# Four gate tiles of a two-group encoder step as two pairs by seven products, with two edits in its attention

## The chip, the cores and the metric

The kernel runs on one core of one Trainium2 chip. The metric is the device time of one execution in microseconds (us). A core has five engines with a queue of instructions each: TensorE (PE, matrix products; its weight loads are shown as PEld), VectorE (DVE), ScalarE (ACT), GpSimd (POOL) and SyncE (SP), which issues the DMAs here. An engine takes its instructions in the order of the program and waits for another through semaphores. PE writes its results to PSUM, which has eight banks; DVE and ACT read them there.

## The reference

Two layers of a streaming encoder work on 1152 tokens: 1024 of a prompt and 8 x 16 of running streams, which also have 256 cached keys and values each. The parts that matter here, for one layer:

```python
h = jnp.einsum('btd,de->bte', x, w_in)
px, pg, q, k, v, ag, ga, gb = jnp.split(h, IN_SPLITS, axis=-1)
...
o = prompt_diff_attention(q, k, v, lam)      # per head: (softmax(q1 k1) - lam * softmax(q2 k2)) v
of = o.astype(jnp.float32)
of = of * lax.rsqrt(jnp.mean(jnp.square(of), -1, keepdims=True) + RMS_EPS)
of = of * subln_w.astype(jnp.float32) * (1.0 - lam_init)
yb = of.astype(x.dtype).reshape(B, T, D_ATT) * jax.nn.silu(ag)
merged = (jax.nn.sigmoid(ga) * jnp.einsum('btc,cd->btd', ya, w_a)
          + jax.nn.sigmoid(gb) * jnp.einsum('btc,cd->btd', yb, w_b))
```

`ag` is the output gate of the attention: 1024 columns, one tile of 128 for each of 8 heads. `ga` and `gb` gate the merge of the two branches, `pg` gates the pooling branch.

## The kernel before

All matrix products of the projections are made in three matmuls on values split into a high and a low part (high x high, high x low, low x high), each over 128 rows of the contraction. A layer has these stages, in this order.

**The V stage** (and, in layer 0, the entry normalisation). It also prepares sums of blocks of x, `t1` to `t4`.

**The pair stage.** `pairs` lists 14 pairs of weight tiles. Two tiles and the two halves of the contraction form a block matrix of 2 x 2; so do the two halves of the contraction and of the tokens. `unit` multiplies them in seven block products in place of eight, for one of two column groups `c` of 288 tokens at a time (`CW`). A block product (`prod`, L595 to L602) is 4 x 3 matmuls of 288 columns, so a pair is 2 x 7 x 12 = 168 matmuls. `keep` and `join` form the sums, and `emit` (L605) finishes a quarter of the result: for a pool gate (`"pg"`) a tanh on ACT, one product on DVE, and a store to DRAM two ticks later. The weights of a pair are added and split in `Weights`, in the order of `plan`.

**The pool stage**: four merge gates (`gates_p2`), the pooling branch, and the product with `w_a`.

**The attention stage.** `attention()` is a generator that goes over `flow`: 8 heads with 9 query tiles each (eight of the prompt, in the order 7, 3, 6, 2, 5, 1, 4, 0, and the decode tile "d"; a tile i has (i+1) x 128 keys). In round j it emits, in this order: the scores of tile j (`s1_tile`, PE into `ps_two`, two buffers; tiles 4 to 7 take one for each map); the transposes of tile j-2 (`s2a_tile`, PE into `bank("tr")`, two buffers, copied to `at` by ACT at L1120); the softmax of tile j (`soft`: DVE's maximum, ACT's exponential); the mix of tile j-1 on DVE (`mix_tile`); the pending squares on ACT; a first `yield f1`; the products of tile j-2 with V (`s2b_tile`) and the copy of its output out of PSUM (`finish`, L1125); a second `yield f2`. For the decode tile `s1_dec`, `mix_dec`, `s2a_dec` and `s2b_dec` take these places.

At each yield the caller emits steps of `filler()`: single steps (three matmuls of 384 columns, L321 to L323, into `bank("lin")`) of the gate tiles in `gate_order`. A tile takes 3 token groups x 8 steps = 24 steps; the last step of a group is followed by ACT's tanh (L975), for the attention's gate by a DVE product (L978), and by a store. How many steps a yield gets is set by

```python
share = (len(gate_order) * NG * KD - REST) / (H * sum(map(sum, STEPS)) + HEAD0)
```

with `NG` 3, `KD` 8, `REST` 28, `H` 8, `HEAD0` 8 and `STEPS` the nine (f1, f2) of a head, 52 in sum. A running sum `due` turns share x f into whole steps. `gate_order` has 16 tiles: the eight of the attention's gate, then eight of `gb`. `g_load` reads a head's gate back from DRAM one head later, for `post_b`.

**The merge stages**: the product with `w_b`, the gating, the product with `w_o` and the normalisation.

Of the kernel before, what the change touches and what calls it, by code (L numbers as in the profile page):

```python
# [11 lines left out]
F32 = mybir.dt.float32  # L12
F32R = mybir.dt.float32r
AF = mybir.ActivationFunctionType
ALU = mybir.AluOpType
AX = mybir.AxisListType

P = 128
# [10 lines left out]
H = 8  # L29
# [3 lines left out]
KD = D // P  # L33
# [7 lines left out]
U_PX, U_PG, U_Q, U_K, U_GA, U_GB, U_AG = 0, 4, 8, 16, 24, 32, 40  # L41
# [23 lines left out]
def trunk(ctx, tc, a):  # L65
    nc = tc.nc
    V, S, G, PE = nc.vector, nc.scalar, nc.gpsimd, nc.tensor
# [3 lines left out]
    small = ctx.enter_context(tc.tile_pool(name="small", bufs=3))  # L71
# [5 lines left out]
    def dr(name, shape):  # L77
        return dram.tile(shape, F32, tag=name, name=name)
# [15 lines left out]
    def later(n, fn):  # L94
        pending.append([n, fn])
# [29 lines left out]
        return t[:, :, g * GW:(g + 1) * GW]  # L125

    gates_p2 = [(2, d) for d in range(KD - MG, KD)]
    gate_order = [(0, d) for d in range(H)] + [(1, d) for d in range(KD)]

    GATE_U = (U_AG, U_GB, U_GA)  # L130
    pairs = []
# [6 lines left out]
        pairs.append(("pg", g, U_PG + g))  # L138
    for d in range(0, KD - MG, 2):
        pairs.append(("ga", d, U_GA + d))  # L140

    plan = []
    for l in range(DEPTH):
# [315 lines left out]
    for l in range(DEPTH):  # L459
# [3 lines left out]
        g_d = dr(f"g_d{l}", [H, P, T])  # L463
# [4 lines left out]
        sg_d = dr(f"sg_d{l}", [4, P, T])  # L468
# [22 lines left out]
        def cols(c, half):  # L491
            o = half * HT + c * CW
            return slice(o, o + CW)
# [35 lines left out]
        for n in range(2 * NT):  # L529
            u, t = n // NT, (TO, TO1)[n // NT][n % NT]  # L530
# [62 lines left out]
        def tt():  # L593
            return p1.tile([P, CW], F32, tag="tt", name="tt", bufs=11)
# [9 lines left out]
        def emit(kind, idx, e, c, half, src, psum):  # L604

            o = cols(c, half)
            if kind == "px":
                if psum:
                    t = tt()
                    S.copy(t, src)  # L610
                    src = t
                g = idx + e
                if half == 1 and c == 1:
                    n = SEQ - o.start
                    later(2, lambda: (dma(u_d[g, :, o.start:SEQ], src[:, :n]),
                                      dma(us_d[g, :, :, HIST:], src[:, n:].rearrange("p (b s) -> p b s", b=DB))))
                    return
                dst = u_d[g, :, o]
            elif kind == "pg":
                t = tt()  # L620
                S.activation(out=t, in_=src, func=AF.Tanh, scale=0.5)
                V.scalar_tensor_tensor(out=t, in0=t, scalar=1.0, in1=src, op0=ALU.add, op1=ALU.mult)
                src, dst = t, sg_d[idx + e, :, o]
            else:
                t = tt() if psum else src
                S.activation(out=t, in_=src, func=AF.Tanh, scale=0.5)
                src, dst = t, ga_d[idx + e, :, o]
            later(2, lambda: dma(dst, src))
# [24 lines left out]
        def unit(kind, idx, c, w, end):  # L653
# [20 lines left out]
            def e2():  # L674
                prod(y_, w["a12"], operand("b21", c), True)
                st[11] = join(y_, s1)
                if kind != "rope":
                    emit(kind, idx, 0, c, 0, st[11], False)
# [9 lines left out]
            def e5():  # L688
                prod(z_, w["s4"], operand("b22", c), False)
                st[12] = join(z_, s2)  # L690
                if kind != "rope":
                    emit(kind, idx, 0, c, 1, st[12], False)
                else:
                    rope(*idx, c, 1, st[12], st[22], False)

            def e6():
                prod(x_, w["s3"], operand("t3", c), False)
                st[22] = join(x_, s5)
                if kind != "rope":
                    emit(kind, idx, 1, c, 1, st[22], False)  # L700
# [20 lines left out]
        for kind, idx, _ in pairs:  # L721
            w = {}
            for c in range(2):
                e = unit(kind, idx, c, w, c == 1)
# [39 lines left out]
        nlam = small.tile([P, 1], F32, tag="nlam", name="nlam", bufs=2)  # L764
# [281 lines left out]
        def start_head(h):  # L1046
            hd = heads[h]
            hd["osb"] = ap.tile([P, 9, P], F32, tag="osb", name="osb", bufs=2)
            hd["ss"] = small.tile([P, 9], F32, tag="ss", name="ss", bufs=2)
            hd["r1"] = small.tile([P, 9], F32, tag="r1", name="r1", bufs=2)  # L1050
            G.memset(hd["r1"][:, 8:9], 1.0)

        def s1_tile(h, i):

# [45 lines left out]
        def mix_tile(h, i):  # L1100
            hd = heads[h]
            pt, ls_ = hd["P", i]
            r2 = small.tile([P, 1], F32, tag="ar2", name="ar2")
            V.reciprocal(out=r2, in_=ls_[:, 1:2])  # L1104
            cc = small.tile([P, 1], F32, tag="acc", name="acc")
            V.scalar_tensor_tensor(out=cc, in0=ls_[:, 0:1], scalar=nlam, in1=r2, op0=ALU.mult, op1=ALU.mult)
            V.scalar_tensor_tensor(out=pt[0], in0=pt[1], scalar=cc, in1=pt[0], op0=ALU.mult, op1=ALU.add)  # L1107
            V.reciprocal(out=hd["r1"][:, i:i + 1], in_=ls_[:, 0:1])

        def s2a_tile(h, i):  # L1110
            hd = heads[h]
# [10 lines left out]
            hd["at", i] = ats  # L1122

        def finish(hd, o_ps, i):
            V.tensor_copy(hd["osb"][:, i, :], o_ps)  # L1125

            def square():
                jk = ap.tile([P, P], mybir.dt.bfloat16, tag="jk", name="jk")
                S.activation(out=jk, in_=hd["osb"][:, i, :], func=AF.Square, accum_out=hd["ss"][:, i:i + 1])

            squares.append(square)
# [3 lines left out]
        def do_squares():  # L1135
            while squares:
                squares.pop(0)()

        def s2b_tile(h, i):
            hd = heads[h]  # L1140
            o_ps = bank("tr")[:, :P]
            for b in range(i + 1):
                PE.matmul(o_ps, hd["at", i][b // 4][:, (b % 4) * P:(b % 4 + 1) * P], hd["vt", b // 4][:, b % 4, :],  # L1143
                          start=(b == 0), stop=(b == i))
            finish(hd, o_ps, i)
            del hd["P", i]
# [54 lines left out]
        def s2b_dec(h):  # L1201
            hd = heads[h]
            atl, vn = hd["atl"], hd["qkv"][2]
            o_ps = bank("tr")[:, :P]
            for uu in range(4):
                PE.matmul(o_ps[32 * uu:32 * uu + 32, :], atl[:, 32 * uu:32 * uu + 32], vn, start=True, stop=False,
                          tile_position=(0, 32 * uu))
            for k in range(2):
                for e in range(2):
                    for uu in range(4):  # L1210
                        g, u = divmod(uu, 2)
                        vcv = hd["vc"][g].rearrange("p (j k v) -> p j k v", j=4, k=2)
                        PE.matmul(o_ps[32 * uu:32 * uu + 32, :],
                                  azt[:, k, uu, e * 32:e * 32 + 32], vcv[:, 2 * u + e, k, :],
                                  start=False, stop=(k == 1 and e == 1), tile_position=(0, 32 * uu))
            finish(hd, o_ps, 8)

        def post_a(h):
            do_squares()
            hd = heads[h]  # L1220
            r1, ss, osb = hd["r1"], hd["ss"], hd["osb"]
            f = small.tile([P, 9], F32, tag="wv_", name="wv_", bufs=2)
            V.tensor_tensor(out=f, in0=r1, in1=r1, op=ALU.mult)
            V.tensor_tensor(out=f, in0=f, in1=ss, op=ALU.mult)
            V.tensor_scalar(out=f, in0=f, scalar1=1.0 / P, scalar2=RMS_EPS, op0=ALU.mult, op1=ALU.add)
            G.tensor_tensor(out=f, in0=f, in1=mhalf[:, :9], op=ALU.pow)
            G.tensor_tensor(out=f, in0=f, in1=r1, op=ALU.mult)
            heads[h]["f"] = f
# [50 lines left out]
        def attention():  # L1279
# [6 lines left out]
            def mix(h, i):  # L1286
                mix_dec(h) if i == "d" else mix_tile(h, i)
# [6 lines left out]
            for j in range(len(flow) + 2):  # L1294
# [4 lines left out]
                if n == 0 and h < H:  # L1299
                    start_head(h)  # L1300
# [18 lines left out]
                if 0 < h < H:  # L1319
                    if n == 2:  # L1320
                        post_a(h - 1)
                        g_load(h - 1, 0)
                        g_load(h - 1, 1)
                    if n == 3:
                        post_f(h - 1)
                    if 5 <= n <= 7:
                        post_b(h - 1, n - 5)
                    if n == 5:
                        g_load(h - 1, 2)
                    if n == 7:  # L1330
                        posted.append(h - 1)
# [9 lines left out]
                if h + 1 < H:  # L1341
# [4 lines left out]
                    if n == 8:  # L1346
                        load_vc(h)
                yield f2
            post_a(H - 1)
            post_f(H - 1)  # L1350
            g_load(H - 1, 0)
# [140 lines left out]
        for n, (d, g) in enumerate(chunks):  # L1492
# [14 lines left out]
            t, u = gates.pop(n)  # L1507
# [25 lines left out]
        dst = a["o_y"] if last else x_d[1]  # L1533
# [46 lines left out]
        if last:  # L1580
            t = TO[-1]
# [133 lines left out]
```

## Time and profile before

| | |
|---|---|
| median of 3 runs | 2343.69 us (2340.68 to 2344.43) |
| the profiled execution, its own time | 2339.09 us |
| its span in the trace | 2336.9 us |
| granted TensorE clock, mean | 0.997 |
| pair stage, layer 0 | 125.5 to 439.7 us of the span |
| pool stage, layer 0 | 439.7 to 553.9 |
| attention stage, layer 0 | 553.9 to 956.1 |
| pair, pool and attention stage, layer 1 | 1282.5 to 1596.5, to 1708.6, to 2111.5 |

The profile is of one execution. Durations in its rows are in us where a row begins with a start time (start, duration, engine, line, operation, output<-inputs, shapes, count), and in groups of instructions "busy us, mean ns | idle us before them, and what ended most of it". A matmul's duration overlaps that of the next one, so for PE the distance between starts is what a matmul costs. A row of waits gives the waiting engine and line, what it waited for, the total, the times and the longest.

### The profile page before, as it was taken

Reading aid. Unit: us, or ns where it says so; the run is one execution under the profiler, and the core shown is the slowest. Engines: PE = TensorE matmul, PEld = TensorE weight load, DVE = VectorE, ACT = ScalarE, POOL = GpSimd, SP = SyncE. Lnnn points to the kernel's source line nnn. Section 1 sums busy time; section 2 is a strip of 40 time slices with the busy share of each in tenths; the row PEclk is TensorE's granted clock in tenths of the full one; section 3 lists DMA queues with packets and bytes.
Section 4 is the critical chain, followed back from the end, with each engine's and each line's share of the span. In section 5 each row is a group of like instructions: output and inputs, shape, how many; then the busy total and the mean of one; then the engine's idle time right before and its main releaser. Section 6 shows DMA issues by size and latency. Waiting matters only on the chain.

```text
span 2336.9 us, 39893 instructions
## 1 busy us (share of the span) xinstructions
PE 2284.7 (98%) x14928; PEld 2148.0 (92%) x14928; DVE 1539.3 (66%) x2980; ACT 982.2 (42%) x2177; POOL 302.0 (13%) x312
## 2 busy tenths in 40 slices
PE   7999999999999999999999999999999999999998
PEld 6899999999989998998878999999999899989986
DVE  4478855446888887566424887556378887874755
ACT  8432234323665665433543332342155565653121
POOL 1023310000000000132100333000000010001333
PEclk9999999999999999999999999999999999999999
DMA  6653334656555554586335432455665464536941
GB/s 216 222 126 103 101 102 115 196 151 197 154 172 156 162 170 146 195 290 230 126 122 198 132 101 100 110 123 181 182 180 157 144 201 149 172 124 220 336 155 73
DMA packets 247714, 379.11 MB, mean 162 GB/s; under 512 B 49888, under 2 KB 190176, under 8 KB 247520
## 3 DMA queue, kind: packets, MB, share of 16 engines
q1 hardware_dynamic: 247520, 376.55, 52.3%
q8 instruction: 118, 1.93, 0.4%
q14 instruction: 76, 0.62, 0.1%
HBM read 259.67 MB, written 117.83 MB: 162 GB/s over the span
## 4 chain that ended last, share of the span: by engine, by line
PE 80%; DMA 7%; DVE 6%; ACT 3%; issue 3%; SPq 1%; POOL 1%; DVEq 0%; ACTq 0%; POOLq 0%
PE ps_lin L321 6%; PE ps_lin L323 6%; PE ps_lin L322 6%; PE ps_tr L1143 5%; PE ps_lin L600 5%; PE ps_lin L602 5%; PE ps_lin L601 5%; PE ps_tr L1118 3%; PE ps_tr L601 2%; PE ps_tr L602 2%; PE ps_tr L600 2%; PE ps_lin L336 2%; PE ps_lin L337 2%; PE ps_lin L335 2%; PE ps_two L1085 2%
## 5 line engine op out<-in xcount | busy, mean ns | idle before, releaser
L321 PE MATMUL ps_lin<-xh,wh 128*128 128x384 f32 x952 | 346.4, 364 | 1.5 <-ACT xh L1266 0.9
L322 PE MATMUL ps_lin<-xl,wh 128*128 128x384 f32 x952 | 321.4, 338 | 1.0 <-DVE xl L1269 1.0
L323 PE MATMUL ps_lin<-xh,wl 128*128 128x384 f32 x952 | 321.3, 338 | 0.0
L321 PEld LDWEIGHTS ps_lin<-xh,wh 128*128 128x128 f32 x952 | 180.5, 190 | 6.7 <-issue 2.2
L322 PEld LDWEIGHTS ps_lin<-xl,wh 128*128 128x128 f32 x952 | 180.7, 190 | 2.9 <-DVE xl L1269 2.4
L323 PEld LDWEIGHTS ps_lin<-xh,wl 128*128 128x128 f32 x952 | 179.6, 189 | 0.0
L1120 ACT COPY at<-ps_tr 128x512 f32<-128x512 f32 (+2 forms) x192 | 86.6, 481 | 191.5 <-PE ps_tr L1118 191.3
L1143 PE MATMUL ps_tr<-vt,at 128*128 128x128 f32 x1152 | 150.0, 276 | 0.0
L1143 PEld LDWEIGHTS ps_tr<-vt,at 128*128 128x128 f32 x1152 | 145.8, 191 | 2.0 <-ACT at L1120 2.0
L271 DVE TENSOR_TENSOR wl<-ws,wh 128x1024 fp32r<-128x1024 f32 (+1 forms) x74 | 86.2, 1164 | 75.0 <-ACT wh L266 74.5
L1093 DVE TENSOR_REDUCE anm<-ps_two 128x1 f32<-128x1024 f32 (+3 forms) x128 | 131.2, 1025 | 4.4
L1095 ACT ACTIVATE p<-ps_two,anm 128x1024 f32<-128x1024 f32 (+3 forms) x128 | 122.2, 961 | 25.4 <-DVE anm L1093 22.2
L266 ACT CAST wh<-ws 128x1024 fp32r<-128x1024 f32 (+1 forms) x74 | 74.1, 1002 | 118.5 <-PE ps_lin L322 50.0
L644 POOL TENSOR_TENSOR tt<-tt 128x288 f32<-128x288 f32 x64 | 63.7, 995 | 408.7 <-DVE tt L643 251.0
L1107 DVE SCALAR_TENSOR_TENSOR p<-p,acc 128x1024 f32<-128x1024 f32 (+7 forms) x128 | 104.9, 819 | 4.5
L1075 ACT ACTIVATE p<-ps_two,anm 128x512 f32<-128x512 f32 (+3 forms) x128 | 66.4, 524 | 79.6 <-DVE ar L1104 59.9
L1118 PE MATMUL ps_tr<-ident,p 128*128 128x128 f32 x576 | 85.6, 274 | 6.3 <-ACT at L1120 4.0
L1085 PE MATMUL ps_two<-kh,qs 128*128 128x512 f32 (+3 forms) x256 | 90.1, 355 | 1.4 <-ACT p L1075 1.2
L1086 PE MATMUL ps_two<-kl,qs 128*128 128x512 f32 (+3 forms) x256 | 89.2, 352 | 1.4 <-DVE kl L909 1.4
L663 ACT COPY sb<-ps_lin 128x288 f32<-128x288 f32 x80 | 31.9, 399 | 123.0 <-PE ps_lin L602 117.5
L1118 PEld LDWEIGHTS ps_tr<-ident,p 128*128 128x128 f32 x576 | 68.7, 141 | 12.1 <-ACT at L1120 5.5
L1511 POOL TENSOR_TENSOR mg<-mt 128x384 f32<-128x384 f32 x42 | 60.1, 1436 | 113.3 <-DVE mt L1510 111.7
(522 smaller groups left out, 6855.9 us busy)
## 6 DMA issues: line engine op xcount, KB each, us to landing
ws<-wt SPq DMA_DIRECT2D x96, 512.0 KB, 3.8
mt_d<-th SPq DMA_DIRECT2D x96, 192.0 KB, 2.9
fx<-q_d SPq DMA_DIRECT2D x128, 128.0 KB, 3.3
fx<-o_k SPq DMA_DIRECT2D x128, 128.0 KB, 3.3
st<-ck SPq DMA_DIRECT2D x32, 512.0 KB, 6.6
fx<-cv SPq DMA_DIRECT2D x32, 512.0 KB, 4.8
mt<-mt_d SPq DMA_DIRECT2D x42, 384.0 KB, 5.9
xT_d<-xs SPq DMA_DIRECT2D x36, 256.0 KB, 2.6
```

The source lines that it names most:

```text
L321: PE.matmul(ps, wh[:, k, :], xh[:, k, :], start=(k == 0), stop=False),
L322: PE.matmul(ps, wh[:, k, :], xl[:, k, :], start=False, stop=False),
L323: PE.matmul(ps, wl[:, k, :], xh[:, k, :], start=False, stop=(k == nk - 1)))
L600: PE.matmul(ps, wh[:, k, :], oh[:, k, :], start=first and k == 0, stop=False, **more)
L601: PE.matmul(ps, wh[:, k, :], ol[:, k, :], start=False, stop=False, **more)
L602: PE.matmul(ps, wl[:, k, :], oh[:, k, :], start=False, stop=k == 3, **more)
L1085: PE.matmul(s[:, b, :c], qs[:, ql], kh[:, kc], start=True, stop=False)
L1093: V.tensor_reduce(out=nm[:, m:m + 1], in_=s[:, :, :c], axis=AX.XY, op=ALU.max, negate=True)
L1095: S.activation(out=p[:, :n].rearrange("p (b c) -> p b c", b=2), in_=s[:, :, :c], func=AF.Exp, bias=nm[:, m:m + 1], accum_out=ls_[:, m:m + 1])
L1107: V.scalar_tensor_tensor(out=pt[0], in0=pt[1], scalar=cc, in1=pt[0], op0=ALU.mult, op1=ALU.add)
L1118: PE.transpose(tr[:, j * P:(j + 1) * P], p[:, (b0 + j) * P:(b0 + j + 1) * P], ident)
L1143: PE.matmul(o_ps, hd["at", i][b // 4][:, (b % 4) * P:(b % 4 + 1) * P], hd["vt", b // 4][:, b % 4, :], start=(b == 0), stop=(b == i))
```

## The change

Four of the eight tiles of the attention's output gate, those of heads 0 to 3, leave `gate_order` and become two more pairs at the end of `pairs`, of the new kind "ag". `emit` treats "ag" like "pg", with `g_d` as the destination. `plan` follows both lists, so the eight weight tiles of both layers are loaded, added and split in the pair stage. `share` gets smaller with the length of `gate_order`; `STEPS`, `REST` and `HEAD0` stay. Beside it `finish` copies the attention's output out of PSUM with ACT in place of DVE, and `mix_tile` takes the reciprocals of both row sums in one instruction of two columns, into a tile `r1` that holds both for every query tile, where there were two instructions, one of them behind the mix.

```diff
-    gate_order = [(0, d) for d in range(H)] + [(1, d) for d in range(KD)]
+    gate_order = [(0, d) for d in range(H // 2, H)] + [(1, d) for d in range(KD)]
...
+    for d in range(0, H // 2, 2):
+        pairs.append(("ag", d, U_AG + d))
...
-            elif kind == "pg":
+            elif kind in ("pg", "ag"):
                 t = tt()
                 S.activation(out=t, in_=src, func=AF.Tanh, scale=0.5)
                 V.scalar_tensor_tensor(out=t, in0=t, scalar=1.0, in1=src, op0=ALU.add, op1=ALU.mult)
-                src, dst = t, sg_d[idx + e, :, o]
+                src, dst = t, (sg_d if kind == "pg" else g_d)[idx + e, :, o]
...
-            hd["r1"] = small.tile([P, 9], F32, tag="r1", name="r1", bufs=2)
-            G.memset(hd["r1"][:, 8:9], 1.0)
+            hd["r1"] = small.tile([P, 9, 2], F32, tag="r1", name="r1", bufs=2)
+            G.memset(hd["r1"][:, 8, 0:1], 1.0)
...
-            r2 = small.tile([P, 1], F32, tag="ar2", name="ar2")
-            V.reciprocal(out=r2, in_=ls_[:, 1:2])
+            rr = hd["r1"][:, i, :]
+            V.reciprocal(out=rr, in_=ls_)
             cc = small.tile([P, 1], F32, tag="acc", name="acc")
-            V.scalar_tensor_tensor(out=cc, in0=ls_[:, 0:1], scalar=nlam, in1=r2, op0=ALU.mult, op1=ALU.mult)
+            V.scalar_tensor_tensor(out=cc, in0=ls_[:, 0:1], scalar=nlam, in1=rr[:, 1:2], op0=ALU.mult, op1=ALU.mult)
             V.scalar_tensor_tensor(out=pt[0], in0=pt[1], scalar=cc, in1=pt[0], op0=ALU.mult, op1=ALU.add)
-            V.reciprocal(out=hd["r1"][:, i:i + 1], in_=ls_[:, 0:1])
...
         def finish(hd, o_ps, i):
-            V.tensor_copy(hd["osb"][:, i, :], o_ps)
+            S.copy(hd["osb"][:, i, :], o_ps)
...
-            r1, ss, osb = hd["r1"], hd["ss"], hd["osb"]
+            r1, ss, osb = hd["r1"][:, :, 0], hd["ss"], hd["osb"]
```

## The prediction

> **What bounds the kernel now.** I read the page of the profile first: its list of engines, then the chain that ended last.
>
> ```profile
> PE 2284.7 (98%) x14928; PEld 2148.0 (92%) x14928; DVE 1539.3 (66%) x2980; ACT 982.2 (42%) x2177; POOL 302.0 (13%) x312
> ...
> PE 80%; DMA 7%; DVE 6%; ACT 3%; issue 3%; SPq 1%; POOL 1%; DVEq 0%; ACTq 0%; POOLq 0%
> ```
>
> TensorE (PE) is busy for 98% of the span and makes 80% of the chain. So the time is the sum of the matmul spacings plus what PE stands still. Next I read the busy time by stretches: the last four pairs of the pair stage of layer 0, two at a time, and the attention stage of layer 0 (layer 1 repeats it).
>
> ```profile
> core 0: us, PE busy (x) PEld busy (x) DVE busy (x) ACT busy (x) POOL busy (x), PEclk, DMA share, GB/s
> 350.37:394.89 44.52, 44.52 (x338) 44.52 (x337) 25.41 (x47) 18.38 (x42) 0.00 (x0) 1.00 0.48 130
> 394.89:439.41 44.52, 44.52 (x337) 44.36 (x336) 14.64 (x26) 16.27 (x37) 0.00 (x0) 1.00 0.48 95
> 553.90:956.10 402.20, 395.82 (x2914) 371.19 (x2913) 319.50 (x781) 232.30 (x615) 18.29 (x23) 1.00 0.53 158
> ```
>
> In the pair stage PE never stands and VectorE (DVE) is busy for 25.41 of 44.52 us at most. In the attention PE stands only 6 us of 402, but DVE is busy for 79% of it, and the gate steps in between are what covers DVE's and ScalarE's (ACT's) answers.
>
> **The change part by part: the gate tiles.** Each moved tile leaves 24 steps of three 384-column matmuls out of the attention. The first matmuls of a step and of the third step after it:
>
> ```profile
> 708.74 0.34 PE L321 MATMUL ps_lin<-xh,wh 128*128 128x384 f32 x1
> ...
> 710.30 0.34 PE L321 MATMUL ps_lin<-xh,wh 128*128 128x384 f32 x1
> ```
>
> A step is (710.30 - 708.74) / 3 = 0.52 us. Eight tiles over two layers are 192 steps: 99.8 us off PE. Added are two pairs a layer. Two pairs took 44.52 us, so four take 89.0 us. The product count alone saves 10.8 us. The added pairs' ACT and DVE work is that of the pool gate pairs, the first of the two pair rows, where both fit under PE; if they didn't fit, the excess over 44.52 us would show, and 19 us are spare. The four weight loads and the stores to `g_d` of a layer go through SP's queue in the pair stage instead:
>
> ```profile
> ws<-wt SPq DMA_DIRECT2D x96, 512.0 KB, 3.8
> ```
>
> One tile's load lands in 3.8 us and a pair needs two in 22 us, at a DMA share of 0.48; I cost them at nothing, hidden by the same 44.52 us. Uncovered, each would cost up to its 3.8 us.
>
> A rule of the Trainium skill speaks against this saving. "TensorE: Matmul & The Clock Gate", Back-to-back issue gap, gives a sustained 81 ns a matmul at 128 columns and 131 ns at 512. An estimate on the line between them is 102 ns at 288 columns and 114 ns at 384; then 672 matmuls for 576 would cost 3 us more. The trace disagrees: 44.52 us over 336 is 132 ns and 0.52 us over three is 173 ns, and I go by these.
>
> **What covers less.** The attention issues its gate steps in shares: before, (16 x 24 - 28) / (8 x 52 + 8) = 0.840 of a unit in STEPS, after, (12 x 24 - 28) / 424 = 0.613. A round of one query tile has 3 to 7 units and loses one step of 0.52 us, sometimes two. The load of the engines follows from these rows of the first attention stage (DVE, then ACT):
>
> ```profile
> L1125 DVE COPY osb<-ps_tr 128x128 f32<-128x128 f32 x71 | 20.1, 283 | 20.0 <-PE ps_tr L1143 19.7
> ...
> L978 DVE SCALAR_TENSOR_TENSOR th<-th,ps_lin 128x384 f32<-128x384 f32 x24 | 13.3, 554 | 15.4 <-ACT th L975 15.3
> ...
> L1108 DVE RECIPROCAL r<-als 128x1 f32<-128x1 f32 x64 | 10.0, 156 | 0.0
> ```
>
> ```profile
> L975 ACT ACTIVATE th<-ps_lin 128x384 f32<-128x384 f32 x45 | 22.0, 489 | 11.6 <-PE ps_lin L323 11.6
> ...
> L1120 ACT COPY at<-ps_tr 128x128 f32<-128x128 f32 x16 | 4.3, 268 | 12.9 <-PE ps_tr L1118 12.9
> ```
>
> DVE loses 72 output copies (20.4 us), 64 reciprocals (10.0) and 12 gate products of 0.554 (6.6): 319.5 - 37.0 = 282.5 us. ACT gains 72 copies; the nearest row is its own copy of that shape, 0.268 us, so 19.3, and loses 12 tanh (5.9): 245.7 us. The splitting of four weight tiles, which both lose too, comes on top. PE's stage becomes 402.2 - 49.9 = 352.3 us. At 80% and 70% neither engine is a bound by its sum. The two-wide reciprocal costs what one costs (a width of one more element; bounds 0.156 and twice that), so the chain to the mix keeps its length. What counts is where PE waits for a single answer.
>
> The tightest place comes once a head: query tile 7, then 3, then the decode tile's second half.
>
> ```profile
> 704.92 1.11 ACT L1095 ACTIVATE p<-ps_two,anm 128x1024 f32<-128x1024 f32 x1
> ...
> 706.63 0.40 PE L1066 MATMUL ps_two<-kh,qs 128*128 128x512 f32 x1
> ...
> 707.29 0.28 DVE L1125 COPY osb<-ps_tr 128x128 f32<-128x128 f32 x1
> ...
> 707.56 0.82 PE L1191 MATMUL ps_tr<-ident,p 128*128 128x128 f32 x6
> ...
> 707.60 0.19 ACT L1129 ACTIVATION_READ_ACCUMULATOR jk<-osb 128x1 f32 x1
> ...
> 711.83 0.68 ACT L1075 ACTIVATE p<-ps_two,anm 128x512 f32<-128x512 f32 x1
> ...
> 713.06 0.37 PE L1085 MATMUL ps_two<-kh,qs 128*128 128x448 f32 x1
> ```
>
> Tile 3's scores start at 706.63, in the PSUM that tile 7's first exponential left at 706.03: 0.60 us to spare, of which one step takes 0.52. The second half of the decode transposes (about 707.89, the fourth of six that start from 707.56 at spacings of some 0.11) needs the bank that the output copy frees at 707.57. On ACT that copy stands in its queue behind both exponentials and the square, which end at 707.79, so it ends at 708.06: 0.17 us too late as things stand, and 0.69 with a step gone. Tile 6's second map at 713.06 needs tile 3's second exponential, done at 712.51: 0.55 to spare, again a step. Behind these waits stands all of PE's queue, the gate steps too, since they come later in program order. I see 0 to 1.3 us a head (nothing, or all of the 11 units x 0.227 = 2.5 steps removed there) and take 0.45, as the waits follow each other and the later ones start from a delayed PE: 16 x 0.45 = 7.2 us.
>
> The second place comes every round, between the transposes and the products with V:
>
> ```profile
> 719.83 0.60 PE L1118 MATMUL ps_tr<-ident,p 128*128 128x128 f32 x4
> ...
> 720.46 0.59 ACT L1120 COPY at<-ps_tr 128x512 f32<-128x512 f32 x1 [0.64 <-PE ps_tr L1118]
> ...
> 721.31 0.94 PE L1143 MATMUL ps_tr<-vt,at 128*128 128x128 f32 x7
> ```
>
> Two steps lie between; the copy ends at 721.05, 0.26 us before its use. One step less leaves PE short by 0.26 us. Counting the shares out over the rounds gives 13 a layer that fall from two steps to one (30 go from three to two, which is enough). That is at most 2 x 13 x 0.31 = 8 us, at least 0; long tiles need only their first copy at once, so I take 5.5. For mixes and smaller waits (0 to 4 us) I take 2.
>
> **What is given back.** DVE's output copy makes PE wait today:
>
> ```profile
> PE ps_tr L1191 <- DVE osb L1125: 2.9, 4, 0.7
> PE ps_tr L1118 <- DVE osb L1125: 2.3, 4, 0.7
> ```
>
> These 5.2 us come where DVE is late with the copy. Where ACT is free by then they go, where its exponentials come first they stay. Between 0 and 5.2 I take 3.5. Fewer DVE instructions ahead of a mix help only where DVE is behind; I add nothing.
>
> **Sum.** -10.8 + 7.2 + 5.5 + 2 - 3.5 = +0.4 us. The profiled execution took 2339.09 us (span 2336.9 and 2.2 around it), below the median 2343.69 and the lowest run, 2340.68; applied to the median this is 2344.1, rounded 2344.
>
> **The rivals.** Case A, the forecast: the saved products are spent in new waits of the attention; -4 to +5 us, 2339 to 2349. For it speak the spare times of 0.26 to 0.60 us against a step of 0.52.
>
> Case B, faster: the waits don't add up, because a PE that waited at one place finds the next answer ready, and because DVE, 37 us a layer lighter, answers sooner. Then half of A's waits remain (7 of 14.7) and the relief is 4.4, nearer its upper bound: -10.8 - 4.4 + 7 = -8, 2336. For it: DVE's copies also hold up DVE itself (20 us idle before them). Against: in the rows above DVE had nothing queued ahead of tile 7's reduction.
>
> Case C, slower: the output copy on ACT decides. It waits in ACT's queue behind the exponentials of the round, so the bank pair of the transposes comes free late in each round of tile 7, and weight casts of 1.05 us get ahead of it in others. It decides wherever the exponentials end later than PE's product with V. Price: 0.7 us a head at the decode transposes in place of the part of it in A, 11 us, with 7 for the V products and the rest, and 3 for tile 6, less 10.8: +10, 2354.
> Case D: the change doesn't save what it says. A 288-column matmul at 149 ns (99.8 us / 672) or more would leave nothing of the saving. The pair rows have 132, in every pair, so only the added pairs themselves could be slower. Without the 10.8 the sum is +11, 2355. The Trainium skill's sustained figures, named above, would have it so, at +14; the rows leave it 0.01.
>
> **How the numbers follow.** Chances: A 0.41, B 0.30, C 0.28, D 0.01. About 0.2%, 4.7 us, is what a measurement of this kernel tells from no change: faster 0.30 from B, same 0.41 from A, slower 0.29 from C and D. With no waits and the full relief the bound is -16, with all the steps of the tight place lost and the upper bounds elsewhere it is 20.8 + 8 + 4 - 10.8 = +22; neither end is likely. For 8 in 10 I reach from 2333 (B and 3 more) to 2356 (C and 2 more).
>
> **What would show it.** The pair stage must be 44.5 us a layer longer, and the attention 40 to 45 us shorter; 50 or more would be B, under 37 C. In the waits of PE, the rows that name DVE's `osb` must be gone, with new ones for ACT's `osb` before the decode transposes, for ACT's `at` before V, and for ACT's `p` before the scores. DVE in the attention should fall to about 280 us and ACT rise to about 243. A pair costing more than 22.3 us, or PE waiting for DVE's mix in most rounds, would make the prediction wrong.

## The result, and the profile after

The changed kernel takes 2366.53 us (median of 4 runs, 2365.35 to 2371.44) against 2342.18 for the kernel before on the same chip: a ratio of 1.0106, with a 95% interval of 1.0091 to 1.0121. It is slower by 1.1%, 24.4 us, and outside the range I gave. The profiled execution took 2367.01 us with a span of 2365.2, which is 28.3 more than the 2336.9 of before. The profiled execution of before was a quick one (2339.09 against the median of 2342.18), so some 4 us of these 28.3 are not part of the difference of the medians. The page of the kernel after, its engines and its chain:

```profile
PE 2296.4 (97%) x15024; PEld 2137.1 (90%) x15024; DVE 1532.4 (65%) x2776; ACT 1024.9 (43%) x2373; POOL 299.0 (13%) x312
...
PE 71%; DVE 9%; DMA 8%; ACT 6%; issue 4%; SPq 1%; POOL 1%; DVEq 0%; ACTq 0%; POOLq 0%
```

PE made up 80% of the chain before and makes up 71% now; DVE went from 6% to 9% and ACT from 3% to 6%. More of the end is set by answers that PE waits for. The busy time by stretches shows where. First the kernel before, layer 0: pair stage, pool stage, then (behind the attention, whose row stands in the prediction) merge stage and product with `w_o`.

```profile
125.50:439.60 314.10, 312.09 (x2353) 311.67 (x2352) 208.91 (x380) 104.02 (x217) 67.32 (x66) 1.00 0.41 110
439.60:553.90 114.30, 112.15 (x620) 107.20 (x619) 62.38 (x94) 26.86 (x44) 0.22 (x2) 1.00 0.66 205
...
956.10:1072.50 116.40, 114.88 (x647) 112.59 (x648) 73.28 (x88) 37.23 (x51) 32.78 (x25) 0.99 0.83 280
1072.50:1282.40 209.90, 205.55 (x938) 169.70 (x937) 89.66 (x123) 90.24 (x163) 14.37 (x20) 1.00 0.47 155
```

The same view of the kernel after: the same five stages of layer 0, the attention among them.

```profile
126.20:486.30 360.10, 356.61 (x2689) 356.11 (x2687) 234.80 (x430) 123.20 (x261) 67.31 (x66) 1.00 0.40 109
486.30:603.70 117.40, 112.84 (x612) 107.91 (x613) 63.11 (x95) 26.40 (x43) 0.22 (x2) 0.99 0.64 198
603.70:966.00 362.30, 354.39 (x2628) 319.32 (x2626) 287.21 (x628) 233.70 (x668) 16.43 (x23) 1.00 0.55 163
966.00:1085.60 119.60, 116.72 (x654) 113.74 (x654) 73.44 (x87) 38.28 (x53) 31.32 (x24) 0.99 0.79 269
1085.60:1297.80 212.20, 206.14 (x937) 169.40 (x937) 91.03 (x124) 90.19 (x163) 15.68 (x21) 1.00 0.47 155
```

The first figure behind the stretch is its length. Both layers together, against the forecast:

| stage (us, both layers) | before | after | difference | forecast |
|---|---|---|---|---|
| pair | 628.2 | 721.7 | +93.5 | +89.0 |
| pool | 226.3 | 232.1 | +5.8 | 0 |
| attention | 805.1 | 726.0 | -79.1 | -99.8 + 11.2 = -88.6 |
| merge | 234.0 | 239.1 | +5.1 | 0 |
| product with `w_o`, layer 0 | 209.9 | 212.2 | +2.3 | 0 |
| entry | 125.5 | 126.2 | +0.7 | 0 |
| sum | | | +28.3 | +0.4 |

By the counts of matmuls in the rows, 286 of the layer's 288 left the attention stage as it is cut here, 8 left the pool stage (the few steps ahead of the first scores) and 7 more are in the merge stage, where the rest of the steps runs. At 0.173 us a matmul the attention's waits are 2 x 286 x 0.173 - 79.1 = 19.9 us net, in place of 11.2 (1.7 of them are a stretch at half clock, shown below); the pool stages lost 5.8 + 2.8 = 8.6 and the merge stages 5.1 - 2.4 = 2.7. So of the miss of 27.9 us about 9 lie in the attention's waits and 19 outside it, where I had put nothing.

**The pairs themselves.** The last full four pairs of the kernel after, two at a time:

```profile
352.73:397.25 44.52, 44.52 (x338) 44.52 (x338) 26.56 (x49) 18.84 (x42) 0.00 (x0) 1.00 0.46 134
397.25:441.77 44.52, 44.52 (x338) 44.52 (x338) 20.21 (x35) 18.77 (x42) 0.00 (x0) 1.00 0.52 107
```

A pair takes 22.26 us, as before, with PE busy throughout. What the pair stage has beyond 89.0 stands at its end. There the first weight tile of the pool stage is rounded by ACT (the cast to `wh`) before PE can use it. Before:

```profile
435.19 1.05 ACT L266 CAST wh<-ws 128x1024 fp32r<-128x1024 f32 x1
...
439.63 0.34 PE L321 MATMUL ps_tr<-xh,wh 128*128 128x384 f32 x1
```

After, in the same place:

```profile
485.22 1.98 ACT L268 CAST wh<-ws 128x1024 fp32r<-128x1024 f32 x2
...
486.31 0.44 PE L323 MATMUL ps_tr<-xh,wh 128*128 128x384 f32 x1 [1.48 <-ACT wh L268]
...
487.57 0.44 PE L325 MATMUL ps_tr<-xh,wl 128*128 128x384 f32 x1 [0.64 <-DVE wl L273]
```

The cast began 4.4 us ahead of its use; now PE waits 1.48 us for it, and 0.64 us for `wl` behind it. The block products read their weights from three buffers each of `wh`, `wl` and `fb`, in turn. Before, the stage's last product reads `fb`, and the last one to read `wh` began at 431.44. After, with 16 x 7 = 112 operands in the turn in place of 98, the last three products (from 479.87 on) hold all three `wh`. The code issues no cast for the next stage in the last three products (the `- 3` of experiment 4), so the cast comes only behind them. PE stands 2.1 us per layer. Then the clock drops: of this stretch of the kernel after, the granted clock is the column of 0.50 behind POOL's.

```profile
488.40:491.80 3.40, 3.40 (x12) 3.40 (x11) 0.25 (x1) 0.53 (x1) 0.00 (x0) 0.50 0.89 270
```

Twelve matmuls in 3.40 us are 0.28 us each where 0.17 is the rule. I call this a half-clock stretch; it loses 1.7 us. Apart from the start and end of the program, the kernel before has two such stretches of 3.4 us (at 983 and 2140) and the kernel after five (488, 997, 1304, 1779, 2168). Three more at half speed are 5.1 us, which lie inside the stage differences of the table: one in a pool (488), one in a pair (1304) and one in an attention stage (1779).

**The attention.** PE's weight loads (PEld) run ahead of its matmuls and meet a wait first. Their waits in the first attention stage, before (waiting engine and line, what it waited for: total us, times, longest):

```profile
PEld ps_tr L1191 <- DVE osb L1125: 2.1, 3, 1.0
...
PEld ps_tr L1118 <- DVE osb L1125: 1.8, 3, 0.9
...
PEld ps_tr L1143 <- ACT at L1120: 1.0, 4, 0.3
```

And after, where the line numbers are one or two higher:

```profile
PEld ps_tr L1144 <- ACT at L1121: 7.1, 19, 0.6
...
PEld ps_two L1087 <- ACT p L1171: 4.5, 7, 0.8
PEld ps_tr L1119 <- ACT osb L1126: 3.3, 7, 0.6
PEld ps_tr L1192 <- ACT osb L1126: 2.4, 7, 0.5
```

The rows that name DVE's `osb` are gone; ACT's `osb`, its `at` before V and its `p` before the scores are there, as the prediction wanted them. The second row was not foreseen: the scores of query tile 7 (L1087) wait for the decode tile's exponentials (L1171) of the head before. This is the place in the kernel before, at the start of the third head:

```profile
646.45 1.05 ACT L907 CAST kh<-fx 128x1024 fp32r<-128x1024 f32 x1
...
651.00 0.57 ACT L1170 ACTIVATE p<-ps_two,dnm 128x384 f32<-128x384 f32 x1
...
651.73 0.39 PE L1085 MATMUL ps_two<-kh,qs 128*128 128x512 f32 x1
...
652.65 0.39 PE L1085 MATMUL ps_two<-kh,qs 128*128 128x512 f32 x1
```

And in the kernel after:

```profile
687.39 1.05 ACT L909 CAST kh<-fx 128x1024 fp32r<-128x1024 f32 x1
...
691.25 0.39 PE L1087 MATMUL ps_two<-kh,qs 128*128 128x512 f32 x1
...
691.94 0.57 ACT L1171 ACTIVATE p<-ps_two,dnm 128x384 f32<-128x384 f32 x1
...
692.66 0.50 PE L1087 MATMUL ps_two<-kh,qs 128*128 128x512 f32 x1 [0.32 <-ACT p L1171]
```

The second map's scores take the PSUM buffer that the decode's exponentials leave. Before, the second exponential ended at 651.57 and PE came for the buffer at 652.65, 1.08 us later. After, PE comes for tile 7 only 2.81 us after the cast of `kh` (from its end at 688.44 to 691.25) in place of 4.23 (647.50 to 651.73), and the exponential ends at 692.51, where PE, with 0.23 us from one of these matmuls to the next, would have come at 692.17. The exponential itself is no later: in both kernels it ends 4.07 us after that cast. What changed is that PE, with fewer steps in its queue, comes earlier.

**Where in a round.** From the starts of the matmuls I worked out, for every round of the attention, the distance from its first scores to the next round's, less 0.5195 us for each gate step in it. What is left is the round's own products plus PE's waits. Means over heads 1 to 6 of both layers, as "steps / us left"; the last three columns are kernels of the experiments below.

| round, its scores | before | after | one pair | other STEPS | placed by round |
|---|---|---|---|---|---|
| tile 7 | 4.0 / 2.26 | 3.0 / 2.84 | 3.7 / 2.44 | 4.0 / 2.90 | 4.0 / 2.54 |
| tile 3 | 5.0 / 3.19 | 3.8 / 3.41 | 4.3 / 3.64 | 5.0 / 3.37 | 5.0 / 3.23 |
| tile 6 | 4.3 / 4.44 | 3.2 / 4.54 | 3.7 / 4.52 | 4.0 / 4.32 | 3.0 / 4.37 |
| tile 2 | 5.8 / 2.04 | 4.0 / 2.27 | 5.2 / 2.07 | 4.0 / 2.05 | 4.0 / 2.08 |
| tile 5 | 4.2 / 3.74 | 3.0 / 3.74 | 3.5 / 3.75 | 3.0 / 3.74 | 2.0 / 3.66 |
| tile 1 | 6.0 / 1.85 | 4.5 / 1.86 | 5.2 / 1.82 | 4.0 / 1.82 | 3.0 / 2.00 |
| tile 4 | 4.0 / 3.59 | 3.0 / 3.65 | 3.5 / 3.79 | 3.0 / 4.08 | 3.0 / 4.65 |
| tile 0 | 5.2 / 1.87 | 3.5 / 2.04 | 4.3 / 2.05 | 3.0 / 2.52 | 3.0 / 2.58 |
| decode | 5.2 / 4.03 | 4.0 / 3.92 | 4.5 / 4.04 | 3.0 / 3.73 | 5.0 / 3.79 |
| a head | 43.7 / 27.01 | 32.0 / 28.27 | 37.9 / 28.12 | 33.0 / 28.53 | 32.0 / 28.90 |

After less before is 1.26 us a head, 20 us if taken for all 16 heads: near the net of the attention above. 0.80 of it is in the rounds of tiles 7 and 3, the tightest place of the prediction.

### The profile page after: what moved, and what is told of

Read it like the earlier page. It is cut to its first block, busy times and chain, and to the rows that moved or that the text cites. A ratio compares the mean times of both kernels' runs of the same rounds, so it can differ in the third digit from the quotient of the medians.

```text
span 2365.2 us, 40170 instructions
## 1 busy us (share of the span) xinstructions
PE 2296.4 (97%) x15024; PEld 2137.1 (90%) x15024; DVE 1532.4 (65%) x2776; ACT 1024.9 (43%) x2373; POOL 299.0 (13%) x312
## 4 chain that ended last, share of the span: by engine, by line
PE 71%; DVE 9%; DMA 8%; ACT 6%; issue 4%; SPq 1%; POOL 1%; DVEq 0%; ACTq 0%; POOLq 0%
PE ps_lin L604 6%; PE ps_lin L602 6%; PE ps_lin L603 6%; PE ps_lin L323 4%; PE ps_lin L324 4%; PE ps_lin L325 4%; PE ps_tr L1144 4%; PE ps_tr L603 3%; PE ps_tr L602 3%; PE ps_tr L604 3%; PE ps_lin L338 2%; PE ps_lin L339 2%; PE ps_lin L337 2%; PE ps_tr L1119 2%; DMA mt_d<-th 1%
## 5 line engine op out<-in xcount | busy, mean ns | idle before, releaser
L323 PE MATMUL ps_lin<-xh,wh 128*128 128x384 f32 x760 | 282.0, 371 | 4.5 <-ACT wh L268 1.5
L324 PE MATMUL ps_lin<-xl,wh 128*128 128x384 f32 x760 | 257.4, 339 | 2.7 <-DVE xl L1270 2.7
L325 PE MATMUL ps_lin<-xh,wl 128*128 128x384 f32 x760 | 257.1, 338 | 0.6 <-DVE wl L273 0.6
L323 PEld LDWEIGHTS ps_lin<-xh,wh 128*128 128x128 f32 x760 | 144.2, 190 | 10.6 <-ACT wh L268 3.5
L324 PEld LDWEIGHTS ps_lin<-xl,wh 128*128 128x128 f32 x760 | 144.8, 191 | 5.2 <-DVE xl L1270 4.7
L325 PEld LDWEIGHTS ps_lin<-xh,wl 128*128 128x128 f32 x760 | 143.6, 189 | 1.0 <-DVE wl L273 1.0
L273 DVE TENSOR_TENSOR wl<-ws,wh 128x1024 fp32r<-128x1024 f32 (+1 forms) x66 | 77.6, 1179 | 68.6 <-ACT wh L268 68.2
L268 ACT CAST wh<-ws 128x1024 fp32r<-128x1024 f32 (+1 forms) x66 | 65.4, 996 | 130.1 <-PE ps_lin L324 53.6
L1087 PE MATMUL ps_two<-kh,qs 128*128 128x512 f32 (+3 forms) x256 | 91.7, 361 | 5.2 <-ACT p L1171 2.5
L665 ACT COPY sb<-ps_lin 128x288 f32<-128x288 f32 x96 | 38.3, 399 | 129.4 <-PE ps_lin L604 125.2
```

The lines of the kernel that those rows point to most:

```text
L323: PE.matmul(ps, wh[:, k, :], xh[:, k, :], start=(k == 0), stop=False),
L324: PE.matmul(ps, wh[:, k, :], xl[:, k, :], start=False, stop=False),
L325: PE.matmul(ps, wl[:, k, :], xh[:, k, :], start=False, stop=(k == nk - 1)))
L1087: PE.matmul(s[:, b, :c], qs[:, ql], kh[:, kc], start=True, stop=False)
```

## The experiments

All ratios are against the kernel before, run on the same chip.

**1. The parts alone.** Three kernels, each with one part of the change on the kernel before. The gate tiles alone (`gate_order`, `pairs`, `emit`):

> Only the four gate tiles are moved to the pair stage; the copy of the attention's output stays on VectorE and both reciprocals stay apart. Theory cover (the steps missing in the attention uncover waits that were hidden, and the pair stage ends with the wrong weight buffers free): nearly all of the 24 us of the whole change stays, 2360 to 2368 us, and the attention stage of layer 0 is 360 to 364 us long, as in the changed kernel (362.3). Theory copy (ScalarE's copy, queued behind exponentials and ahead of casts, is what uncovers the waits): the attention falls to 352 to 356 us and the time to 2340 to 2352 us.

2372.56 us, ratio 1.0134 (1.0115 to 1.0152), above both expectations. Its profiled attention stages, 363.4 and 365.7 us, are 1 to 2 us longer than the changed kernel's: the cover theory's sign. The output copy alone:

```diff
-            V.tensor_copy(hd["osb"][:, i, :], o_ps)
+            S.copy(hd["osb"][:, i, :], o_ps)
```

> Only the copy of the attention's output moves from VectorE to ScalarE; the gate tiles stay in the attention. Theory cover: the 5.2 us that TensorE waits for VectorE's copy go and little comes in their place, 2337 to 2343 us. Theory copy: 5 us or more of new waits a layer, 2350 to 2357 us, with ScalarE's output copy named among the waits of TensorE.

2338.03 us, ratio 0.9984 (0.9974 to 0.9993). Its waits in the first attention stage:

```profile
PEld ps_tr L1118 <- ACT osb L1125: 1.7, 3, 0.9
...
PEld ps_tr L1191 <- ACT osb L1125: 1.3, 5, 0.5
```

They stand where DVE's `osb` stood with 1.8 and 2.1: the copy is waited for a little less, not no longer. Each attention stage is 1.0 us shorter. The reciprocals alone:

```diff
-            V.reciprocal(out=r2, in_=ls_[:, 1:2])
+            V.reciprocal(out=rr, in_=ls_)
...
-            V.reciprocal(out=hd["r1"][:, i:i + 1], in_=ls_[:, 0:1])
```

> Only the two reciprocals become one of two columns. Both theories: 20 us of VectorE's work in two attentions go, none of it is on TensorE's way; 2339 to 2343 us, no difference that can be measured.

2342.54 us, ratio 1.0008 (0.9998 to 1.0018): no difference. So the loss is all with the gate tiles, and the copy on ACT, taken alone, is a small gain. Beside the moved tiles the two small edits together make the ratio 1.0106 in place of 1.0134; experiment 5 comes back to this.

**2. Both small edits without the gate tiles.**

> The second and third edit together, without the move of the gate tiles: ScalarE copies the outputs and one reciprocal serves both maps. Theory: the 3.6 us that the copy alone brings stay and the reciprocals add at most 1 us: 2335 to 2339 us. If the edits lived off each other (a lighter VectorE needed for the copy to help), 2330 to 2334 us.

2338.93 us, ratio 0.9983 (0.9974 to 0.9992). This version beats both kernels, by 0.17% and by 1.2%.

**3. The two halves of the move, apart.** On the kernel of experiment 2, the two pairs are added, with results that go to a tile in DRAM that nobody reads, and the attention keeps its 16 tiles:

```diff
+    for d in range(0, H // 2, 2):
+        pairs.append(("ag", d, U_AG + d))
...
+        gx_d = dr(f"gx_d{l}", [H // 2, P, T])
...
+                src, dst = t, (sg_d if kind == "pg" else gx_d)[idx + e, :, o]
```

> Copies on ScalarE, one reciprocal, and the two added pairs a layer as in the change, but the attention also keeps its own four gate tiles (made twice; the pairs' results are stored to a place that nobody reads). This leaves the attention's cover whole. If the change loses its time in the thinner attention alone, the pairs cost their 89 us and no more over the kernel with the two small edits (2338): 2426 to 2429 us. Theory that the added pairs also bring waits of their own at the end of the pair stage, in the pool stage and in the clock, about 12 us of the 39 found: 2435 to 2441 us, and the attention stage stays at 401 to 403 us.

2439.93 us, ratio 1.0408 (1.0391 to 1.0425), 101.0 us above experiment 2. Four pairs are 89.0, so 12.0 are other costs of the pairs; the attention is as long as before (401.4 and 402.6). Then the other half: the four tiles leave the attention and no pairs are added. The gates of heads 0 to 3 are left out, and these heads read those of heads 4 to 7.

```diff
-    gate_order = [(0, d) for d in range(H)] + [(1, d) for d in range(KD)]
+    gate_order = [(0, d) for d in range(H // 2, H)] + [(1, d) for d in range(KD)]
...
-            dma(t, g_d[h, :, g * GW:(g + 1) * GW])
+            dma(t, g_d[h if h >= H // 2 else h + H // 2, :, g * GW:(g + 1) * GW])
```

> Copies on ScalarE, one reciprocal, and four gate tiles a layer left out of the attention, but not made in the pair stage either: heads 0 to 3 take the gates of heads 4 to 7, so the output gate of those heads isn't computed. The steps save 99.8 us. Theory cover: the attention is 362 us long as in the changed kernel and gives back some 22 us with the merge stage behind it, 2338 - 99.8 + 20 to 26 = 2258 to 2264 us. Rival, that the attention's waits come from the added pairs (later loads, the clock): 2338 - 99.8 + 0 to 8 = 2238 to 2246 us.

2264.9 us, ratio 0.9663 (0.9648 to 0.9677), 74.0 below experiment 2, where the steps taken out are worth 99.8; this is 0.9 above the cover theory's range and far from the rival's. The attention stages are 39.6 and 37.4 shorter than before, as in the changed kernel, though nothing was added elsewhere. The halves add up: 2338.9 + 101.0 - 74.0 = 2365.9 against 2366.5 measured. So some 26 us are lost because steps leave the attention, and some 12 because pairs come in; the product count gives 10.8 back.

**4. The wait at the pool's start.** The next stage's weights may be split during the last products of the pair stage too, where this stopped three products ahead of the end (`- 3` to `- 1`):

```diff
-                if n < len(order) - 3:
+                if n < len(order) - 1:
```

> The changed kernel, with the weights of the pool stage allowed to be split in the last three products of the pair stage (before, the splitting stopped three products ahead of its end). Theory that the turn of the weight buffers costs the start of the pool stage: the 1.5 and 0.6 us waits of TensorE at its start go in both layers, and the half clock behind them in layer 0, 4 to 8 us in all: 2358 to 2363 us. Rival, that the casts only take the place of other work on ScalarE there, or that the pool stage is longer for another reason: 2364 to 2368 us.

2365.61 us, ratio 1.0103 (1.0088 to 1.0118), the same as without. The pair stages are now 44.3 and 45.0 longer than before, so the wait at their end is gone. But this row of PE's waits is new:

```profile
PE ps_lin L789 <- DVE pl L822: 3.6, 1, 3.6
```

In the first pool stage the wait moved 15 us on, to the pooling branch, whose differences `pl` come late, and the clock halves there for 6.8 us. The pair stage's excess can be taken away without a gain that shows: in that stage what is late next is the pool's input.

**5. The copy, with the gate tiles moved.** The changed kernel with `V.tensor_copy` in `finish`, as before.

> The changed kernel without its ScalarE copy: the attention's output is copied by VectorE again, gate tiles moved and reciprocals joined. Theory that the copy on ScalarE decides (it waits behind the exponentials, more so where steps are missing): without it the time falls from 2366 to below 2360. Cover theory (steps missing, whoever copies): the copy on ScalarE helps here as it does without the moved tiles, where it gave 3.6 us; so 2369 to 2374, PE's waits for VectorE's osb back and longer than the 5.2 us of before.

2367.43 us, ratio 1.0107 (1.009 to 1.0125): the changed kernel has 1.0106. Both expectations missed. The copy on ACT does not make it slower, which case C of the prediction needs, but the 3.6 us that it gives alone are no longer seen either. In the attention of this kernel, with the copy on DVE:

```profile
PEld ps_tr L1144 <- ACT at L1121: 7.7, 19, 1.2
...
PEld ps_two L1087 <- ACT p L1171: 4.5, 7, 0.8
```

The two largest waits are there with nearly the same totals (7.1 and 4.5), so they don't come from the copy's place in ACT's queue. This kernel differs from the first of experiment 1 by the reciprocals alone, and the ratios are 1.0107 and 1.0134. That the joined reciprocals are worth some 6 us beside the moved tiles, and nothing without them, is possible but not shown: the two intervals overlap, and the attention stages of the two profiles differ by only 0.7 and 0.6 us.

**6. Half the dose.** One pair in place of two: only the tiles of heads 0 and 1 move.

```diff
-    gate_order = [(0, d) for d in range(H // 2, H)] + [(1, d) for d in range(KD)]
+    gate_order = [(0, d) for d in range(2, H)] + [(1, d) for d in range(KD)]
...
-    for d in range(0, H // 2, 2):
+    for d in range(0, 2, 2):
```

> The changed kernel with one pair in place of two: only the gate tiles of heads 0 and 1 become a pair, 14 tiles stay in the attention. The share of a step at each yield is (14 x 24 - 28) / 424 = 0.726, between 0.840 and 0.613. The two small edits alone give before - 3.5 us, both pairs on top of them +27.6. Linear theory (every moved step uncovers as much as the one before, and each pair costs its own disturbance): -3.5 + 13.8 = +10.3, 2350 to 2355 against 2342. Threshold theory (answers were covered with some 0.26 to 0.6 us to spare, so that the first steps taken away cost little and the last ones much): the products save 5.4, the attention's waits are a quarter of 22 and not half, the pair stage's own costs at most half of 7: about -3.5 - 5.4 + 5.5 + 3.5 + 2 = +2, 2340 to 2347. A gain of over 6 us would say that one pair is the better dose.

2358.44 us, ratio 1.0071 (1.0052 to 1.009): slower than either theory had it. The stages around the pairs are undisturbed: the pair stages are 22.3 and 22.1 longer than before and the pool stages 1.7 and 0.5 shorter. But the attention stages are only 15.9 and 17.2 shorter, where 48 steps each are worth 25.0: 9.1 and 7.8 us of waits, against 10.0 and 10.7 with twice as many steps gone (1.7 of the 9.1 and of the 10.7 are a half-clock stretch each). Most of the attention's loss comes with the first half. (The profiled execution took 2354.48 us and was the fastest of the four, so that some 4 us of the median's loss aren't in these stages.) Its waits in the first attention stage:

```profile
PEld ps_tr L1192 <- ACT osb L1126: 4.0, 5, 1.9
PEld ps_two L1068 <- ACT p L1097: 4.0, 5, 1.7
PEld ps_tr L1119 <- ACT at L1121: 2.7, 3, 0.9
```

These are the two waits that the prediction named for its tightest place, tile 3's scores and the decode transposes. With two pairs, PE has already waited for tile 7's buffer, and the two are down to 1.3 and 2.4.

**7. The same steps, placed otherwise.** Two attempts on the changed kernel. The first gives whole steps, two before each product with V, and 12 more of them to the attention:

```diff
-STEPS = [(2, 3), (5, 1), (3, 2), (3, 4), (3, 2), (3, 4), (3, 2), (3, 3), (3, 3)]
+STEPS = [(2, 2), (4, 1), (2, 2), (2, 2), (2, 1), (2, 2), (2, 1), (2, 1), (2, 1)]
...
-REST = 28
+REST = 16
```

> The changed kernel with its attention steps placed elsewhere: (2, 2), (4, 1), (2, 2), (2, 2), (2, 1), (2, 2), (2, 1), (2, 1), (2, 1) for the nine rounds of a head at one step a unit, so two steps or more always stand before the products with V and nine in the rounds of tiles 7 and 3; 272 steps in the attention in place of 260. Theory cover: the waits before V fall from 7.1 us a layer (on the weight-load queue of TensorE) to under 2, those for tile 3's and the decode tile's exponentials shrink, and the time falls to 2352 to 2360 us. Rival, that the answers come late wherever the steps stand, since the chain of VectorE and ScalarE is what bounds a head: 2363 to 2370 us.

2385.71 us, ratio 1.0178 (1.0158 to 1.0199), slower than both theories said. The wait before V did go, from 7.1 to 1.7 us in the first attention stage, but others grew, this one most:

```profile
PEld ps_two L1068 <- ACT p L1097: 6.8, 8, 2.0
```

By the counts of matmuls each attention stage got 10 more steps (5.2 us) and is 3.9 and 3.4 us longer, so its waits are 1.3 and 1.8 smaller. But the merge stages have 14 steps less (7.3 us) and are still 1.0 and 2.1 longer: PE now stands 3.0 us where the attention ends, in both layers, and each merge stage has two half-clock stretches more, 3.4 us. The steps left over were covering that passage. The second attempt, after the table by rounds, nearly keeps the number of steps (264 a layer against 262) and gives the most to the decode round and the fewest to that of tile 5:

```diff
+STEPS = [(2, 2), (4, 1), (2, 1), (2, 2), (2, 0), (2, 1), (2, 1), (2, 1), (3, 2)]
...
+HEAD0 = 5
+REST = 27
```

> The changed kernel with the same number of gate steps in the attention (261 of 288 against 260), but each yield gets whole steps, the same in every head, placed by what the traces so far lost in each round: five behind the decode scores, the fewest (2 and 0) in the round of tile 5, which lost nothing at 3. Only STEPS, HEAD0 and REST differ. Placement theory (the shares fall on the wrong yields; where they fall right, most waits go): each attention stage 5 to 8 us shorter than the changed kernel's 362 and 364, 2351 to 2358 in all. Cover theory (32 steps a head are too few for the answers of the other engines wherever they stand, so that a wait taken from one place comes up at another): attention within 3 us of the changed kernel's, 2362 to 2371. Neither reaches before's 2342, since some 14 us of the loss lie outside the attention.

2378.94 us, ratio 1.0158 (1.0137 to 1.0178), slower than both theories said. The attention stages are 5.8 and 7.1 longer than the changed kernel's; 3.4 of these 12.9 us are two half-clock stretches more, and 2.1 two steps in each. In the table the rounds that got steps improved (tile 7 from 2.84 to 2.54, tile 3 from 3.41 to 3.23), and tile 4 and tile 0 lost more (3.65 to 4.65 and 2.04 to 2.58), tile 4 with as many steps in its own round as in the changed kernel: the two rounds ahead of it had lost theirs. The wait of tile 3's scores is the largest again, 8.5 us in the first attention stage. Two placements by hand are worse than the scaled shares. That no better one exists is not shown by two.

## Why the prediction was wrong

**Right: the prices of the work.** A moved tile's steps took 0.52 us and a pair 22.26, as costed; the saving of 10.8 by products is real, and case D fell. By the prediction's estimate from the sustained figures in the Trainium skill's "TensorE: Matmul & The Clock Gate", Back-to-back issue gap, the added pairs would have cost more than the steps they replace; the 44.52 us rows for the new pairs disagree, at 132 ns a matmul against 173 in a step. The two-wide reciprocal takes 155 ns where the one-wide took 156, and alone changes nothing in the time. The relief by ACT's copy, taken as 3.5, was 3.6 where it was the only edit.

**Wrong first: "I cost them at nothing, hidden by the same 44.52 us".** That holds for the loads. It asked only whether the new work fits under PE, and not what the next stage finds when it begins. Experiment 3 prices this side at 12.0 us with two pairs; experiment 6 finds no such cost in the pair and pool stages with one. In the changed kernel the pair stages have 4.5 us beyond the 89.0 and the pool stages 8.6: 4.2 of these 13.1 are the waits at the pool's start in both layers, and 3.4 two half-clock stretches. Most of the other 5.5 stands in PE's waits later in the pool stages, for `pl`, `th` and `sg` from DVE and ACT: 3.9 and 2.8 us, against 2.1 and 0.4 before. Why these come later stays open. The range had no bound for any of it.

**Wrong second: the size of the tight place, "0 to 1.3 us a head ... take 0.45".** The rounds of tiles 7 and 3 lost 0.80 us a head, 12.8 in place of 7.2. The bound held and the mechanism was right, that the spare time there is about a step. But the first to be late was the score product of tile 7 behind the decode's exponentials, one answer ahead of the three that I priced. The spare time there was 1.08 us, which I had not read.

**Wrong third: the smaller waits and the relief.** 5.5 + 2 - 3.5 = 4.0 was the forecast for the rest of the rounds; it came to 0.46 a head, 7.4. The waits before V were there as named. The relief did not come: by experiment 5 the copy on ACT gives nothing that shows once the steps are gone.

**The signs.** The pair stages became 46.0 and 47.5 us longer, not 44.5. The attention became 39.9 and 39.2 us shorter, and the prediction called 40 to 45 right. This sign was badly set: the sum itself gives 44.3, and the lower end of 40 already meant waits of 10 a layer, nearly twice the sum's. DVE in the attention came to 287 us and ACT to 234, where the sign said 280 and 243; neither is a bound, and I did not follow up the difference.

**The rivals.** Case B (waits don't add up) fell: their net sum was nearly twice the forecast. It was right in one thing, as experiment 6 shows: a PE that waited at one place finds the next answer ready, so that the second half of the steps adds little to the waits of the first. I had this work towards a small total; it works from a large first half. Case C had the sign, but not for its reason: ACT's copy is no loss alone (experiment 1) or with the tiles moved (experiment 5).

**Open.** The merge stages' 2.7 us and the 2.3 of the product with `w_o` were not separated; the latter stage differs by 2.2 between the kernel before and the copy alone as well, where its work is the same. How much of the attention's loss a better placement would give back is open too. Only one dose between none and two pairs was run, and that its first half costs most is read from the stages of one profile.

## What to carry to other kernels

Steps that fill an in-order engine's queue are worth their own time only until the first answer behind them is late, so read the spare time of every answer in a round before taking any out, and don't expect the first ones taken to be free: here the first half uncovered most of the waits. When work moves into another stage, its price there isn't its duration alone: work out which buffers the stage now ends on, and what the next stage needs in its first microseconds. Edits that stand beside a large one should be timed apart from it; here the two small ones gain 0.17% by themselves, inside a change that loses 1.1%.

## What was not expected of the hardware

A single wait of 1.48 us, and one of 0.64 us 1.3 us later, in a stage where PE is otherwise busy without a gap, was followed by 3.4 us at a granted clock of 0.50. It isn't certain to follow: the same waits at the start of the pool stage of layer 1 (1659.4) have no such stretch behind them, and a wait of 2.0 us at the start of layer 1's pair stage has one after the change and none before. All single stretches seen in these runs between the program's start and end last 3.4 us, the two long ones 6.8. Their starts lie on a grid: those of the kernel after are 149, 90, 139 and 114 times 3.413 us apart, and the other traces with more than one have whole multiples too. On this grid the two waits of layer 0 fall into the one window that ends at 488.4, and those of layer 1 into two windows:

```profile
484.99:488.40 3.41, 1.45 (x7) 1.13 (x8) 2.57 (x3) 2.21 (x3) 0.00 (x0) 1.00 0.25 87
1655.77:1659.18 3.41, 2.16 (x17) 1.93 (x15) 1.83 (x4) 1.60 (x3) 0.00 (x0) 1.00 0.24 87
1659.18:1662.59 3.41, 2.53 (x13) 2.21 (x14) 2.36 (x2) 1.13 (x2) 0.00 (x0) 1.00 0.34 93
```

PE stood 1.96 us of the first window, and 1.25 and 0.88 of the other two. In all thirteen traces, from the pair stage of layer 0 to the last 15 us, every window in which PE stood more than 1.9 us by its records was followed by a half-clock stretch. Between 1.6 and 1.9 us some were and some weren't, and in the merge stages stretches also follow windows with only about 1.1. So whether a wait of 1.5 to 2 us costs another 1.7 depends on where it falls on the grid. The Trainium skill, "TensorE: Matmul & The Clock Gate", Why this matters for your kernels, asks for no gaps above some 3 us between bursts of matmuls; here gaps of half that length were followed by the lower clock, and the measurement decides. The same page (What's actually happening) has the clock set in free-running windows of about 3.4 us, with which the length and the grid of the stretches agree.

A copy of 128x128 out of PSUM took 283 ns on DVE before and 261 on ACT after, a difference of 0.022 us a copy. Moving the copies gave 3.6 us where it was the only edit, and nothing that shows where the gate tiles had left the attention.
